# Rope columns by halves in DRAM, the swap on VectorE out of PSUM, and whole splits of the query and rope key weights

## The chip, the cores and the metric

The kernel runs on one core of one Trainium2 chip. The metric is the device time of one execution in microseconds. Before the change it was 1918.83 us, the median of three runs (1917.03 to 1919.51).

## What is computed

A decoder trunk of two layers on 256 tokens of width 2048. Layer 0 is a causal pooling mixer with a SwiGLU feed-forward network. From its result a key/value set is made once: a compressed latent of rank 512, 16 heads of keys and values of 128 columns each, and one rotary key of 64 columns that all heads share. Layer 1 is attention on that set, with low-rank queries, and a second feed-forward network. Shift, scale and gate of each sub-layer come from products of a conditioning vector with large matrices.

Of the reference, the parts that the change touches:

```
def apply_rope(t, cos, sin):
    half = t.shape[-1] // 2
    t1, t2 = t[..., :half], t[..., half:]
    return jnp.concatenate([t1 * cos - t2 * sin, t2 * cos + t1 * sin], axis=-1)

k_rope = apply_rope(h @ w_kr, cos, sin)                  # (S, 64)
q = (cq @ w_uq).reshape(B, S, N_HEADS, 128 + 64)
q_nope = q[..., :128]
q_rope = apply_rope(q[..., 128:], cos[:, :, None, :], sin[:, :, None, :])
s = q_nope @ k_nope.T + q_rope @ k_rope.T                # by head, causal, scaled, softmax
```

## The kernel before

All weights stream once from DRAM through six buffers ("raw", 8 KB a partition), nearly always as tiles of 1 MB. To keep fp32 accuracy each weight is split in two: ScalarE copies it to an upper half in fp32r (`split`, line 374), VectorE subtracts to get the lower half (line 376), and TensorE multiplies upper by upper, upper by lower and lower by upper (`proj_unit`, line 398, and `head_T`, line 1288). The loads go out on SP's queue; a raw buffer is free for the next load when VectorE has read it.

The products with the conditioning vector run in the background, on VectorE alone: one pass over a 1 MB tile with a row sum (`Part.unit`, line 211). A counter (`tick`, line 342) decides after how many weight tiles the next pass is issued: `split` counts, and so does `project_heads`, by a call of its own (line 1355). In the attention 1.5 passes go out for each of the query groups 2 to 7. When a gate's 16 passes are done, `gate_to` adds the bias (line 300) and puts a small job on the list `pending`: a transpose on TensorE (line 292), a copy on ScalarE, a DMA issued by ScalarE and one issued by POOL. The list is worked off by `flush`, which `split` calls behind its two instructions. The query split of line 1362 does not call `split`, and so does not flush.

The rope key is made at the end of `then_attention`, in a stretch whose order on TensorE, ScalarE and VectorE is written out by hand (lines 1199 to 1227). `w_kr` is loaded in rows of 64 columns (line 1176). ScalarE copies it twice, side by side, into `wkr_h` (line 1201), four subtractions make `wkr_l` (line 1217), and the matmuls of line 1208 leave the 64 rows of the rope key twice in PSUM. Then `rope_start` follows. The tables `cos_t` and `sin_t` have a row for each partition; the sign of the sine lies in a column of constants (line 81).

`rope_start` (line 840) takes the 128 x 256 product out of PSUM with ScalarE: one copy as it is (line 843) and four copies of 32 partitions each with the halves swapped (line 845). `rope_end` (line 848) multiplies the swapped one by the sine (line 849) and the other by the cosine (line 850) and adds them (line 852). For the rope key the sum goes to `krT` in two pieces of 64 partitions, one for each head of a pair, with zeros around them.

The attention works in 8 groups of two heads. `project_heads(g)` (line 1342) loads the group's columns of `w_uq`, 512 x 384 (line 1354), splits the 128 rope columns and then the 256 others, each with one ScalarE and one VectorE instruction (lines 1362 and 1363), makes the rope product with 12 matmuls (lines 1368 to 1370), calls `rope_start`, and makes the two heads' queries with 24 matmuls (line 1288). Its `finish` calls `rope_end`. In the loop at line 1448 a group runs through `probabilities` (scores on TensorE, lines 1383 to 1386; scale and mask, line 1390 on VectorE and 1388 on ScalarE; maximum, line 1393; exponentials on ScalarE, lines 1396 and 1397; reciprocal on VectorE, line 1399; the scaling by it on ScalarE, line 1400, and on VectorE, line 1401). Meanwhile the probabilities of the group before are transposed on TensorE (line 1407), copied out (line 1409) and multiplied with the values (lines 1414 and 1415), with `project_heads(g + 2)` between the two. The order of the instructions on each engine is here not written out: a scheduler puts them in order when the program is built, by their place in the program, by raised priorities (`tc.high_priority`) and by its own estimate of when each can start. On the chip each queue then keeps that order.

Of the kernel before, what the change touches and what calls it, by code (L numbers as in the profile page):

```python
# [9 lines left out]
F32 = mybir.dt.float32  # L10
# [7 lines left out]
P = 128  # L18
T = 256
# [54 lines left out]
def shape_constants():  # L74
# [6 lines left out]
    con[:, C_SIGN] = np.where(q % ROPE < HALF, -1.0, 1.0)  # L81
# [12 lines left out]
def tile_trunk(ctx: ExitStack, tc: tile.TileContext, a: dict, out: bass.AP):  # L94
# [712 lines left out]

    cos_t = const.tile([P, T], F32, name="cos_t")
# [31 lines left out]
    def rope_start(bank):  # L840

        t_ = t2k([P, 2, T])
        act.activation(t_[:, 0, :], bank, AF.Copy)
        for r in range(0, P, HALF):
            act.activation(t_[r:r + HALF, 1, :], bank[r ^ HALF:(r ^ HALF) + HALF], AF.Copy)
        return t_

    def rope_end(t_, dsts):
        dve.tensor_tensor(out=t_[:, 1, :], in0=t_[:, 1, :], in1=sin_t, op=ALU.mult)
        dve.tensor_tensor(out=t_[:, 0, :], in0=t_[:, 0, :], in1=cos_t, op=ALU.mult)  # L850
# [271 lines left out]
    def then_attention(old, banks, piece):  # L1122
# [49 lines left out]
        for j in range(2, ND):  # L1172
            w_ = w_load_of(dkv(j))
            if j == 2:
                wkr = raw_t([P, KD, ROPE])
                sync.dma_start(wkr, a["w_kr"].rearrange("(k p) n -> p k n", p=P))
# [22 lines left out]
        wkr_h, wkr_l = hl_t([P, KD, 2, ROPE]), hl_t([P, KD, 2, ROPE])  # L1199
        for i in range(2):  # L1200
            act.activation(wkr_h[:, :, i, :], wkr, AF.Copy)
# [3 lines left out]
        def key_part(n):  # L1205
            w_, i = sums[n]
            for k in range(KD):
                pe.matmul(krb[:, :T], lhsT=w_[:, k].rearrange("p i n -> p (i n)"), rhs=hkv[k // KL][:, i, k % KL, :],
# [6 lines left out]
        for ks in (slice(0, KD // 2), slice(KD // 2, KD)):  # L1215
            for i in range(2):
                dve.tensor_tensor(out=wkr_l[:, ks, i, :], in0=wkr[:, ks], in1=wkr_h[:, ks, i, :].bitcast(F32),
                                  op=ALU.subtract)
# [97 lines left out]
    rope_end(kr_t, [(slice(0, ROPE), krT[0:ROPE, 0, :]), (slice(ROPE, P), krT[ROPE:P, 1, :])])  # L1316
# [20 lines left out]
    w_uq = a["w_uq"][0]  # L1337
# [4 lines left out]
    def project_heads(g):  # L1342
        o = Heads()
        n = HG * T
        if g % 2 == 0:
# [8 lines left out]
        sync.dma_start(rq, w_uq[:, g * HG * QH:(g + 1) * HG * QH].rearrange("(k p) n -> p k n", p=P))  # L1354
        tick()
        q_h, q_l = ([t_[:, :KL * HG * NOPE].rearrange("p (k h n) -> p k h n", k=KL, h=HG),
                     t_[:, KL * HG * NOPE:].rearrange("p (k h n) -> p k h n", k=KL, h=HG)]
                    for t_ in (hl_t([P, KL * HG * QH]), hl_t([P, KL * HG * QH])))
        src = rq.rearrange("p k (h n) -> p k h n", h=HG)
# [218 lines left out]
```

## Time and profile before

| | |
|---|---|
| median of three runs | 1918.83 us (1917.03 to 1919.51) |
| the profiled execution: its time | 1918.19 us |
| its span, first to last instruction | 1916.4 us |
| mean granted TensorE clock | 0.987 |
| TensorE busy | 1862.8 us, 97% |
| VectorE busy | 1402.7 us, 73% |
| ScalarE busy | 850.2 us, 44% |

The profile is of one execution. Busy is the time in which an engine has an instruction of its own at work; PE is TensorE, PEld its weight loads, DVE VectorE, ACT ScalarE, SP the engine whose queue issues the loads. L1407 is line 1407 of the kernel. A row of the timeline begins with its start and its length in us; a wait stands behind it in brackets, with what ended it. Names such as `ps<-act,hl` are the tiles written and read. [...]

### The profile page before, as it was taken

What the parts mean: (1) busy time and instruction counts of PE and PEld (TensorE: products, weight loads), DVE (VectorE), ACT (ScalarE), POOL (GpSimd) and SP (SyncE); (2) the same over time, 40 slices, a digit from 0 to 9 for tenths busy, and PEclk for the clock granted to TensorE, in tenths of its full rate; (3) what the DMA queues carried; (4) which work ended last, traced back from release to release, by engine and by line L of the source; (5) the groups of instructions that cost most, each with busy time, mean ns of one, the idle gap of its engine ahead of it and who ended that gap; (6) DMA issues with size and microseconds to landing.
All of it is one profiled execution on the core that took longest, in us unless ns stands there. A gap on an engine that the chain in (4) does not pass through costs nothing.

```text
span 1916.4 us, 21930 instructions
## 1 busy us (share of the span) xinstructions
PE 1862.8 (97%) x8813; PEld 1507.8 (79%) x8813; DVE 1402.7 (73%) x1391; ACT 850.2 (44%) x958; POOL 26.9 (1%) x32
## 2 busy tenths in 40 slices
PE   7689999999999999999999999999999999999998
PEld 3255888888888888887889888888888888888887
DVE  2148799999788777799899966889785556645556
ACT  3125643444433334244678745634444433343343
POOL 0000000000000000002100000000000000000000
PEclk9789999999999999999999999999999999999999
DMA  9999998879998888897597775988776666665651
GB/s 399 398 418 417 368 364 333 319 299 361 357 344 332 327 330 326 332 373 274 212 371 291 293 278 194 397 318 335 260 284 240 241 240 239 249 222 205 220 198 44
DMA packets 86647, 574.98 MB, mean 300 GB/s; under 512 B 10977, under 2 KB 15505, under 8 KB 18321
## 3 DMA queue, kind: packets, MB, share of 16 engines
q1 hardware_dynamic: 86018, 570.42, 77.8%
q0 software_dynamic: 432, 3.15, 0.4%
q8 instruction: 69, 1.13, 0.2%
q14 instruction: 32, 0.26, 0.0%
q10 hardware_dynamic: 96, 0.02, 0.0%
HBM read 567.24 MB, written 6.32 MB: 299 GB/s over the span
## 4 chain that ended last, share of the span: by engine, by line
PE 69%; issue 22%; DMA 3%; DVE 3%; ACT 1%; SPq 0%; POOL 0%; POOLq 0%; DVEq 0%; ACTq 0%
PE ps L398 58%; DMA raw<-in_mod_w_dram 3%; PE ps L256 2%; PE ps L973 2%; PE ps L407 2%; PE ps L1288 2%; DVE raw L211 1%; PE ps L729 1%; PE ps L1197 1%; PE ps L540 0%; DMA raw<-in_mod_block_dram 0%; PE ps L196 0%; PE ps L948 0%; PE ps L770 0%; DVE hl L376 0%
## 5 line engine op out<-in xcount | busy, mean ns | idle before, releaser
L398 PE MATMUL ps<-hl,act 128*128 128x512 f32 x6744 | 1539.5, 390 | 1.9 <-DVE hl L376 1.0
L398 PEld LDWEIGHTS ps<-hl,act 128*128 128x128 f32 x6744 | 1263.0, 188 | 264.7 <-DVE hl L376 1.8
L376 DVE TENSOR_TENSOR hl<-raw,hl 128x2048 fp32r<-128x2048 f32 x289 | 661.1, 2289 | 253.2 <-ACT hl L374 252.5
L374 ACT ACTIVATE hl<-raw 128x2048 fp32r<-128x2048 f32 x289 | 553.1, 1918 | 647.8 <-PE ps L398 572.1
L211 DVE SCALAR_TENSOR_TENSOR raw<-raw,s_row 128x2048 f32<-128x2048 f32 x168 | 383.2, 2284 | 3.6 <-DMA raw<-in_mod_wt_dram 3.6
L256 PE MATMUL ps<-raw,s_strip 128*32 128x512 f32 x392 | 65.2, 760 | 34.6 <-DMA raw<-in_mod_w_dram 33.5
L698 DVE TENSOR_TENSOR act<-ps,act 128x512 f32<-128x512 f32 x96 | 64.5, 685 | 17.5 <-PE ps L398 17.5
L256 PEld LDWEIGHTS ps<-raw,s_strip 128*32 128x32 f32 x392 | 9.5, 121 | 70.0 <-DMA raw<-in_mod_w_dram 46.3
L784 DVE TENSOR_TENSOR x<-ps,x 128x512 f32<-128x512 f32 x32 | 22.1, 690 | 38.8 <-PE ps L398 38.8
L1288 PE MATMUL ps<-act,hl 128*128 128x256 f32 x384 | 49.6, 287 | 0.0
L1288 PEld LDWEIGHTS ps<-act,hl 128*128 128x128 f32 x384 | 48.3, 195 | 0.7 <-DVE act L1253 0.2
L407 PE MATMUL ps<-hl,act 128*128 128x512 f32 x192 | 47.0, 400 | 1.2 <-DVE act L503 1.2
L732 ACT ACTIVATE act<-ps 128x512 fp32r<-128x512 f32 x44 | 23.6, 594 | 50.0 <-PE ps L729 37.6
L407 PEld LDWEIGHTS ps<-hl,act 128*128 128x128 f32 x192 | 35.2, 188 | 10.7 <-ACT act L490 2.3
L263 DVE COPY t2k<-ps 128x256 f32<-128x256 f32 x4 | 1.7, 425 | 52.9 <-ACT t2k L262 52.9
L427 ACT ACTIVATE junk<-x 128x512 bf16<-128x512 f32 x23 | 14.5, 629 | 53.2 <-DVE x L612 37.6
L802 DVE TENSOR_TENSOR t2k<-ps,t2k 128x512 f32<-128x512 f32 x24 | 16.5, 689 | 28.5 <-PE ps L398 28.5
L798 ACT ACTIVATE t2k<-ps 128x512 f32<-128x512 f32 x24 | 14.2, 590 | 47.9 <-PE ps L398 47.9
L973 PEld LDWEIGHTS ps<-act,act 128*128 128x128 f32 x128 | 24.7, 200 | 11.6 <-issue 8.4
L696 ACT ACTIVATE act<-ps 128x512 f32<-128x512 f32 x32 | 19.1, 597 | 29.0 <-PE ps L398 28.8
L973 PE MATMUL ps<-act,act 128*128 128x256 f32 x128 | 31.9, 402 | 0.0
L733 DVE TENSOR_TENSOR act<-ps,act 128x512 fp32r<-128x512 f32 x44 | 28.1, 683 | 0.9 <-ACT act L732 0.9
(222 smaller groups left out, 911.6 us busy)
## 6 DMA issues: line engine op xcount, KB each, us to landing
raw<-in_mod_wt_dram SPq DMA_DIRECT2D x136, 1024.0 KB, 5.8
raw<-in_ffn_gate_dram SPq DMA_DIRECT2D x88, 1024.0 KB, 5.8
raw<-in_ffn_up_dram SPq DMA_DIRECT2D x88, 1024.0 KB, 5.1
raw<-in_ffn_down_dram SPq DMA_DIRECT2D x88, 1024.0 KB, 5.2
raw<-in_mod_w_dram SPq DMA_DIRECT2D x48, 1024.0 KB, 12.1
raw<-in_kv_mod_wt_dram SPq DMA_DIRECT2D x32, 1024.0 KB, 7.1
raw<-in_w_o_dram SPq DMA_DIRECT2D x16, 1024.0 KB, 6.1
raw<-in_mod_block_dram SPq DMA_DIRECT2D x8, 1024.0 KB, 12.5
```

Of the source, the lines that this page charges most:

```text
L211: dve.scalar_tensor_tensor(out=r, in0=r, scalar=1.0, in1=s_row, op0=ALU.mult, op1=ALU.mult, accum_out=self.sums[:, self.n:self.n + 1])
L256: pe.matmul(self.bank[m * STRIP:(m + 1) * STRIP, :], lhsT=weights(k), rhs=r[:, k, i, :], start=first, stop=last)
L374: hi_ins = act.activation(hi, r, AF.Copy)
L376: lo_ins = dve.tensor_tensor(out=lo, in0=r, in1=hi.bitcast(F32), op=ALU.subtract)
L398: pe.matmul(banks[tok], lhsT=t_[:, i, k, tok * P:(tok + 1) * P], rhs=w[:, k, :], start=first and n < len(part), stop=last and n >= len(ord ...
L407: pe.matmul(bank, lhsT=t_[:, i, k, tok * P:(tok + 1) * P], rhs=w[:, k, :], start=first and n == 0, stop=last and n == len(order) - 1)
L698: dve.tensor_tensor(out=part, in0=banks[tok], in1=part, op=ALU.add)
L732: act.activation(m[:, 0, :, ts_], v, AF.Copy)
L733: dve.tensor_tensor(out=m[:, 1, :, ts_], in0=v, in1=m[:, 0, :, ts_].bitcast(F32), op=ALU.subtract)
L784: dve.tensor_tensor(out=x[:, tok, js], in0=banks[tok], in1=x[:, tok, js], op=ALU.add)
L973: pe.matmul(mixed[g][:, n % 2, :], lhsT=wp[g][:, k, ns], rhs=pool_all[g // 2][:, g % 2, k, :], start=k == 0, stop=k == KL - 1)
L1288: pe.matmul(pt[:, h, :], lhsT=w(h0 + h, k), rhs=t_[:, i, k, :], start=n == 0, stop=n == 3 * KL - 1)
```

## The change

Five things change together.

- **Layout in DRAM.** `w_uq` is laid out by groups of two heads, each group with one contiguous run for a partition. Inside a group the 128 rope columns come first, ordered by halves: the first 32 of head 0, the first 32 of head 1, then the second 32 of head 0 and of head 1. `w_kr` has each half twice, 128 columns in all, and one contiguous run for a partition; it is twice as large as before.
- **Rope.** With this order the swap of halves is a swap of partitions 0 to 63 with 64 to 127. `rope_start` is now on VectorE: two products of 64 partitions with the sine, straight from PSUM, each written to the other half of the partitions, and one product of all partitions with the cosine. `rope_end` keeps the addition alone. The sign of the sine moves to the row that is read.
- **The rope key's addition** is in four pieces of 32 partitions.
- **The rope key's weights** are copied to the upper half by one ScalarE instruction and subtracted by two VectorE instructions.
- **The query weights** go through `split`: one ScalarE and one VectorE instruction of 128 x 1536, the count by `tick` and the `flush` behind them.

```diff
-    con[:, C_SIGN] = np.where(q % ROPE < HALF, -1.0, 1.0)
+    con[:, C_SIGN] = np.where(q < ROPE, 1.0, -1.0)
...
     def rope_start(bank):
         t_ = t2k([P, 2, T])
-        act.activation(t_[:, 0, :], bank, AF.Copy)
-        for r in range(0, P, HALF):
-            act.activation(t_[r:r + HALF, 1, :], bank[r ^ HALF:(r ^ HALF) + HALF], AF.Copy)
+        for r in range(0, P, ROPE):
+            other = slice(r ^ ROPE, (r ^ ROPE) + ROPE)
+            dve.tensor_tensor(out=t_[r:r + ROPE, 1, :], in0=bank[other], in1=sin_t[other], op=ALU.mult)
+        dve.tensor_tensor(out=t_[:, 0, :], in0=bank, in1=cos_t, op=ALU.mult)
         return t_

     def rope_end(t_, dsts):
-        dve.tensor_tensor(out=t_[:, 1, :], in0=t_[:, 1, :], in1=sin_t, op=ALU.mult)
-        dve.tensor_tensor(out=t_[:, 0, :], in0=t_[:, 0, :], in1=cos_t, op=ALU.mult)
         for rows, dst in dsts:
             dve.tensor_tensor(out=dst, in0=t_[rows, 0, :], in1=t_[rows, 1, :], op=ALU.add)
...
-                wkr = raw_t([P, KD, ROPE])
-                sync.dma_start(wkr, a["w_kr"].rearrange("(k p) n -> p k n", p=P))
+                wkr = raw_t([P, KD, P])
+                sync.dma_start(wkr.rearrange("p k n -> p (k n)"), a["w_kr"])
...
-        wkr_h, wkr_l = hl_t([P, KD, 2, ROPE]), hl_t([P, KD, 2, ROPE])
-        for i in range(2):
-            act.activation(wkr_h[:, :, i, :], wkr, AF.Copy)
+        wkr_h, wkr_l = hl_t([P, KD, P]), hl_t([P, KD, P])
+        act.activation(wkr_h, wkr, AF.Copy)
...
         for ks in (slice(0, KD // 2), slice(KD // 2, KD)):
-            for i in range(2):
-                dve.tensor_tensor(out=wkr_l[:, ks, i, :], in0=wkr[:, ks], in1=wkr_h[:, ks, i, :].bitcast(F32),
-                                  op=ALU.subtract)
+            dve.tensor_tensor(out=wkr_l[:, ks], in0=wkr[:, ks], in1=wkr_h[:, ks].bitcast(F32), op=ALU.subtract)
...
-    rope_end(kr_t, [(slice(0, ROPE), krT[0:ROPE, 0, :]), (slice(ROPE, P), krT[ROPE:P, 1, :])])
+    rope_end(kr_t, [(slice(r, r + HALF), krT[r:r + HALF, r // HALF % 2, :]) for r in range(0, P, HALF)])
...
         rq = raw_t([P, KL, HG * QH])
-        sync.dma_start(rq, w_uq[:, g * HG * QH:(g + 1) * HG * QH].rearrange("(k p) n -> p k n", p=P))
-        tick()
...
-        with tc.high_priority(offset=100):
-            for i, ns in ((1, slice(NOPE, QH)), (0, slice(0, NOPE))):
-                act.activation(q_h[i], src[:, :, :, ns], AF.Copy)
-                dve.tensor_tensor(out=q_l[i], in0=src[:, :, :, ns], in1=q_h[i].bitcast(F32), op=ALU.subtract)
+        sync.dma_start(rq.rearrange("p k n -> p (k n)"), w_uq[g])
+        q_h, q_l = split(rq, [P, KL, HG * QH])
         qb = ps_t()
         for k in range(KL):
-            wh, wl = (w[1][:, k].rearrange("p h n -> p (h n)") for w in (q_h, q_l))
+            wh, wl = (w[:, k, :P] for w in (q_h, q_l))
...
         t_ = rope_start(qb[:, :T])
-        head_T(o.qT, HG, lambda h, k: q_h[0][:, k, h, :], lambda h, k: q_l[0][:, k, h, :], cqT)
+        nope = [slice(HG * ROPE + h * NOPE, HG * ROPE + (h + 1) * NOPE) for h in range(HG)]
+        head_T(o.qT, HG, lambda h, k: q_h[:, k, nope[h]], lambda h, k: q_l[:, k, nope[h]], cqT)
```

## Rows read from the trace of the kernel before

**Rows 1.** The page, part 1: busy us, share of the span, instructions.

```profile
PE 1862.8 (97%) x8813; PEld 1507.8 (79%) x8813; DVE 1402.7 (73%) x1391; ACT 850.2 (44%) x958; POOL 26.9 (1%) x32
```

**Rows 2.** Busy time by stretch: rope key to latent, attention. Columns in the first line.

```profile
core 0: us, PE busy (x) PEld busy (x) DVE busy (x) ACT busy (x) POOL busy (x), PEclk, DMA share, GB/s
926.00:1009.90 83.90, 83.86 (x503) 74.06 (x502) 76.28 (x86) 63.64 (x102) 4.13 (x4) 1.00 0.85 325
1009.90:1080.00 70.10, 67.71 (x491) 64.42 (x490) 67.41 (x146) 60.06 (x160) 0.00 (x0) 0.98 0.79 286
```

**Rows 3.** Waits of TensorE, 1003 to 1100 us: total, times, longest.

```profile
PE ps L1407 <- ACT t2k L1400: 2.2, 2, 2.0
```

**Rows 4.** Timeline, 1026 to 1031 us, VectorE and TensorE.

```profile
1027.82 2.29 DVE L211 SCALAR_TENSOR_TENSOR raw<-raw,s_row 128x2048 f32<-128x2048 f32 x1
...
1030.03 0.16 DVE L1399 RECIPROCAL sm<-sm 128x2 f32<-128x2 f32 x1
...
1030.81 0.55 PE L1407 MATMUL ps<-con,t2k 128*128 128x128 f32 x3 [1.97 <-ACT t2k L1400]
```

**Rows 5.** Busy time and granted clock behind that wait, columns as in rows 2.

```profile
1031.50:1035.50 4.00, 4.00 (x23) 4.00 (x23) 4.00 (x10) 3.31 (x12) 0.00 (x0) 0.57 0.81 305
```

**Rows 6.** Timeline, 1048 to 1051 us: the same step in a later group.

```profile
1049.14 0.40 ACT L1400 ACTIVATE t2k<-t2k,sm 128x128 f32<-128x128 f32 x1
...
1049.81 0.82 PE L1407 MATMUL ps<-con,t2k 128*128 128x128 f32 x6
```

**Rows 7.** Timeline, the load of the rope key's weights and its first reader.

```profile
890.39 0.38 SPq L1176 DMA_DIRECT2D raw<-in_w_kr_dram  x1
...
927.79 2.02 ACT L1201 ACTIVATE hl<-raw 128x1024 fp32r<-128x1024 f32 x2
```

**Rows 8.** Groups of VectorE by shape: count, busy us, mean ns, idle before.

```profile
L376 DVE TENSOR_TENSOR hl<-raw,hl 128x2048 fp32r<-128x2048 f32 x289 | 661.1, 2289 | 253.2 <-ACT hl L374 252.5
L1363 DVE TENSOR_TENSOR hl<-raw,hl 128x1024 fp32r<-128x1024 f32 x8 | 9.8, 1219 | 0.0
L668 DVE TENSOR_TENSOR x<-x,t2k 128x512 f32<-128x512 f32 x8 | 5.5, 692 | 0.3
L667 DVE TENSOR_TENSOR t2k<-ps,gate 128x512 f32<-128x512 f32 x8 | 5.5, 688 | 5.9 <-PE ps L398 3.2 <-PE ps L407 2.7
...
L1363 DVE TENSOR_TENSOR hl<-raw,hl 128x512 fp32r<-128x512 f32 x8 | 5.5, 685 | 0.0
L849 DVE TENSOR_TENSOR t2k<-t2k,sin_t 128x256 f32<-128x256 f32 x9 | 3.8, 419 | 0.6 <-ACT t2k L845 0.5
...
L852 DVE TENSOR_TENSOR krT<-t2k 64x256 f32<-64x256 f32 x2 | 0.8, 414 | 0.0
```

**Rows 9.** Timeline: lower halves on VectorE and the matmuls that read them.

```profile
940.52 4.49 DVE L376 TENSOR_TENSOR hl<-raw,hl 128x2048 fp32r<-128x2048 f32 x2
...
949.84 5.92 PE L1288 MATMUL ps<-act,hl 128*128 128x256 f32 x48
...
1051.82 1.22 DVE L1363 TENSOR_TENSOR hl<-raw,hl 128x1024 fp32r<-128x1024 f32 x1
...
1068.42 0.36 PE L1368 MATMUL ps<-act,hl 128*128 128x256 f32 x1
```

**Rows 10.** DMA issues by line: count, KB each, median us to landing.

```profile
raw<-in_w_uq_dram SPq DMA_DIRECT2D x8, 768.0 KB, 6.3
```

**Rows 11.** Groups of ScalarE by shape, columns as in rows 8.

```profile
L845 ACT ACTIVATE t2k<-ps 32x256 f32<-32x256 f32 x36 | 13.5, 375 | 0.5
...
L843 ACT ACTIVATE t2k<-ps 128x256 f32<-128x256 f32 x9 | 3.4, 375 | 3.8 <-PE ps L1370 2.1 <-ACT t2k L1409 0.9 <-PE ps L1208 0.8
```

**Rows 12.** Timeline of VectorE: two pairs of instructions, one behind the other.

```profile
968.69 0.84 DVE L852 TENSOR_TENSOR krT<-t2k 64x256 f32<-64x256 f32 x2
...
984.64 0.75 DVE L560 TENSOR_TENSOR act<-t2k,act 128x256 fp32r<-128x256 f32 x2
```

**Rows 13.** Timeline: the attention's gate is summed, and later turned.

```profile
1065.22 0.17 DVE L300 TENSOR_TENSOR cols<-sums,vcol 128x16 f32<-128x16 f32 x1
...
1082.10 0.27 PE L292 MATMUL ps<-con,cols 128*16 128x128 f32 x1
```

**Rows 14.** Waits of ScalarE, 1003 to 1100 us, columns as in rows 3.

```profile
ACT t2k L843 <- PE ps L1370: 2.1, 3, 1.2
```

More of the change, by code (lines that the diff above doesn't have):

```diff
@@ L1207, in key_part @@
             for k in range(KD):
-                pe.matmul(krb[:, :T], lhsT=w_[:, k].rearrange("p i n -> p (i n)"), rhs=hkv[k // KL][:, i, k % KL, :],
+                pe.matmul(krb[:, :T], lhsT=w_[:, k], rhs=hkv[k // KL][:, i, k % KL, :],
                           start=n + k == 0, stop=n == 2 and k == KD - 1)
@@ L1336, in tile_trunk @@
     HG = 2
-    w_uq = a["w_uq"][0]
+    w_uq = a["w_uq"]
     class Heads:
@@ L1353, in project_heads @@
         rq = raw_t([P, KL, HG * QH])
-        sync.dma_start(rq, w_uq[:, g * HG * QH:(g + 1) * HG * QH].rearrange("(k p) n -> p k n", p=P))
-        tick()
[L1356 to L1359, printed above, removed]
-        with tc.high_priority(offset=100):
-            for i, ns in ((1, slice(NOPE, QH)), (0, slice(0, NOPE))):
-                act.activation(q_h[i], src[:, :, :, ns], AF.Copy)
-                dve.tensor_tensor(out=q_l[i], in0=src[:, :, :, ns], in1=q_h[i].bitcast(F32), op=ALU.subtract)
+        sync.dma_start(rq.rearrange("p k n -> p (k n)"), w_uq[g])
+        q_h, q_l = split(rq, [P, KL, HG * QH])
         qb = ps_t()
         for k in range(KL):
-            wh, wl = (w[1][:, k].rearrange("p h n -> p (h n)") for w in (q_h, q_l))
+            wh, wl = (w[:, k, :P] for w in (q_h, q_l))
             pe.matmul(qb[:, :T], lhsT=wl, rhs=cqT[:, 0, k, :], start=k == 0, stop=False)
@@ L1544, in columns @@
         return np.asarray(v).reshape(-1, P).T
-    o = {n: np.asarray(i[n]) for n in ("x", "c", "positions", "mod_w", "pool_w", "w_kr", "w_uq", "final_norm")}
+    o = {n: np.asarray(i[n]) for n in ("x", "c", "positions", "mod_w", "pool_w", "final_norm")}
     o["vectors"] = np.concatenate([columns(i[n]) for n in (
@@ L1552, in laid_out @@
     o["mod_block"] = block.transpose(0, 2, 1, 3, 4).reshape(KD // 2, P, 4 * CH)
+    w = np.asarray(i["w_uq"])[0].reshape(KL, P, H // 2, 2, QH)
+    rope = w[..., NOPE:].reshape(KL, P, H // 2, 2, 2, HALF).swapaxes(3, 4).reshape(KL, P, H // 2, 2 * ROPE)
+    w = np.concatenate([rope, w[..., :NOPE].reshape(KL, P, H // 2, 2 * NOPE)], 3)
+    o["w_uq"] = w.transpose(2, 1, 0, 3).reshape(H // 2, P, -1)
+    w = np.asarray(i["w_kr"]).reshape(KD, P, 2, 1, HALF)
+    o["w_kr"] = np.concatenate([w, w], 3).reshape(KD, P, P).transpose(1, 0, 2).reshape(P, KD * P)
     for n in ("w_dkv", "w_uk", "w_uv"):
```

## The prediction

> **What bounds the kernel now.** I read the page's busy times first: TensorE has work in 97% of the span, VectorE in 73%, ScalarE in 44% [rows 1]. So a part of this change can only matter where TensorE waits, or where another engine is nearly as full. The busy times by stretch find that place [rows 2]. From the rope key to the last query latent (926 to 1009.9 us) TensorE is busy for 83.86 of 83.90 us, and nothing that feeds it is late. In the attention, from the first query matmul to the last scores (1009.9 to 1080 us), TensorE is busy for 67.71 of 70.10 us and VectorE for 67.41: two engines are full at once, and ScalarE has 10 us to spare.
>
> TensorE's waits there come to 2.2 us in two, the longest 2.0, both for the scaled probabilities of line 1400 [rows 3]. The timeline shows the long one: VectorE works in the order of its queue, a background pass of 2.29 us (line 211) stands before the reciprocal of the second head, that starts at 1030.03, ScalarE's scaling follows it, and TensorE's transposes go on at 1030.81 after 1.97 us [rows 4]. [...] Elsewhere the chain is only just in time: in a later group ScalarE's last scaling begins at 1049.14, lasts 0.40, and TensorE turns the probabilities at 1049.81, a slack of 0.27 us [rows 6].
>
> **The change part by part.** I follow the order of the program.
>
> *Rope key's weights.* Their load grows from 512 to 1,024 KB. It is issued at 890.39 us and first read at 927.79 [rows 7]; at the 325 GB/s of the stretch that follows [rows 2] half a megabyte more is 1.6 us. The loads queued behind it on SP are as early. Without that cover of 37 us, 1.6 us would show. One ScalarE copy replaces two and two subtractions replace four, with the same elements: nothing.
>
> *Rope key itself.* Its three products now stand in VectorE's written order, ahead of the two lower halves at 940.52 us; they replace two products that ran later, and at the end four additions replace two. Three products at 0.42 [rows 8] and 0.27 for starts that can't overlap (below) put 1.5 us ahead of those two subtractions. The second one ended at 945.0; TensorE takes it from 949.84 on [rows 9]. That lead of 4.8 us hides 1.5; if it were gone, 1.5 us would show. The additions feed only the attention's scores. Nothing.
>
> *Query weights' loads.* Eight loads of 768 KB with 6.3 us to landing [rows 10] keep bytes, queue and place; only the pieces grow: nothing. Without their lead, a landing that is longer or shorter by a part of 6.3 us would show.
>
> *Query weights' split.* Before, each group costs VectorE 685 + 1,219 ns, less an overlap of some 0.09 (below). One subtraction of 1,536 elements lies halfway between 1,219 (1,024) and 2,289 (2,048): 1.75 us [rows 8]. That gives back 0.07 us a group. The rope product now waits for the whole split instead of its first third, at most 1.75 - 0.69 = 1.1 us later; but the splits run ahead of TensorE: the last is over at 1053.04, and its matmuls begin at 1068.42 [rows 9].
>
> *Query rope, ScalarE.* Five copies go: 375 + 4 x 375 ns = 1.9 us a group, 15 us in all [rows 11]. ScalarE is not what is full, and waits for it in the attention are what VectorE's order leaves, so I count no gain.
>
> *Query rope, VectorE.* Before: two products and an addition. After: two half products, a whole one and the addition, so one instruction of 0.42 more, as a 128 x 256 product takes 419 ns and half the partitions take no less (the rope key's 64-partition additions take 414) [rows 8]. The source is now PSUM. The nearest rows are lines 667 and 668, the same operation and size from PSUM and from SBUF: 688 and 692 ns [rows 8]; I count no surcharge. [...]
>
> Then the starts. Two subtractions of 128 x 256, one behind the other, take 0.75 us where two of 0.42 would take 0.84, so they overlap by 0.09. The rope key's two additions, one at partition 0 and one at 64, take 0.84 for 2 x 0.414: no overlap [rows 12]. The new products change their start partition three times in a row, so up to 3 x 0.09 = 0.27 us a group. [...]
>
> Sum for a group: 0.42 + 0.27 - 0.07 = 0.62 us, and 0.35 without the held starts. Eight groups: 5.0 us, at the lowest 2.8. I take 5.0, since the pair at partitions 0 and 64 is the nearest row. The 15 us that ScalarE loses are of another engine and pay for none of it.
>
> *The gate's rows.* The split function also sends out pending work, which the old query split did not. The attention's gate is summed at 1065.22 and turned on TensorE only at 1082.10 [rows 13], with the first output weights. The last query group's split will now send it: one 0.27 us matmul, a ScalarE copy, a DMA issue on ScalarE's queue and one on POOL's, about 15 us earlier. Their lengths stay, ScalarE has the room and POOL has nothing to do there [rows 2]. Zero if TensorE meets it after the sum; if it stands in front of a late sum, TensorE waits up to the lateness of VectorE, at most the 5.0 us above. I take zero and leave the end for the range.
>
> **Sum.** VectorE's 67.41 us in the attention become 72.4, and the stretch lasts 70.10. The 2.69 us in which it idles can be filled only in part, but if they were filled altogether the stretch still grows by 2.3 us. Outside the attention nothing. The profiled execution took 1918.19 us (span 1916.4, and 1.8 around it), 0.64 below the median of 1918.83. 1918.19 + 2.3 = 1920.5 us.
>
> **The rivals.** (a) *The background slides.* The passes of line 211 have no reader in the attention. If as much as one (2.29 us) lands behind it, VectorE's extra work is absorbed and the time stays at 1918.2. For it: in the split, VectorE is 15 us ahead of TensorE [rows 9]. Against: the passes are as old in the program as the split beside them, and at 1027.82 one came ahead of urgent work.
>
> (b) *The late reciprocal goes.* With other lengths the queue is put in another order, and the pass at 1027.82 may land behind the reciprocal: the wait, its clock and the short second wait of 0.2 us [rows 3] go: 1.97 + 1.72 + 0.2 = 3.9 less, 1914.3 us. For it: one instruction decides, and ScalarE is freed. Against: VectorE is fuller, not emptier.
>
> (c) *VectorE waits for TensorE, slower.* The first product stands in VectorE's in-order queue before the query product is done. On ScalarE the copy of line 843 waited so 2.1 us in three places, the longest 1.2 [rows 14]. Queued behind the wait are now the softmax of the previous group, the next split and a pass whose buffer the SP queue needs for the next load. Once such a wait exceeds the slack of 0.27 us [rows 6], the transposes start late; with the 2.3 of the forecast it makes 2.3 + 2.1 = 4.4, and a gap as long as that at 1028.84 costs the clock again: + 1.72. That is 6.1 us, 1924.3.
>
> (d) *The held starts don't come.* If products from PSUM overlap at their changed starts, the sum is its lower end of 2.8, and the stretch grows by 67.41 + 2.8 - 70.10 = 0.1 us: 1918.3, the same outcome as (a).
>
> **How the numbers follow.** Forecast 0.36, (a) with (d) 0.20, (b) 0.17, (c) 0.27. A measurement of this kernel can tell about 0.2%, 3.8 us, from no change: under 1915.0 counts as faster, over 1922.7 as slower. Only (b) is below, only (c) above; so 0.17, 0.56, 0.27. The time is the forecast's, 1920.5. The range takes in (b)'s 1914.3 and (c)'s 1924.3 with some of the gate's end: 1914.0 to 1925.0, leaving out a second long gap.
>
> **What would show it.** Right: three products of 0.42 us per rope from PSUM with no overlap between them, one 1.75 us subtraction a group, ScalarE's busy time down by 15 us, VectorE over 71 us between the first query matmul and the last scores, and that stretch 2 to 3 us longer in waits for line 1400 or 1409. Wrong: the stretch shorter with granted clock 1.00 throughout (b); VectorE idle on TensorE's query matmuls (c); products of clearly more than 0.45 us; or any change of TensorE's waits before 1009 or after 1100 us.

## The result, and the profile after

The changed kernel takes 1920.78 us (median of 22 runs, 1919.25 to 1923.18) against 1918.51 for the kernel before beside it (22 runs, 1914.82 to 1920.38). The ratio is 1.0014, interval 1.0008 to 1.0021: 1.5 to 4.0 us slower, and the ratio is within the 0.2% that was called no change. The forecast of 1920.5 is met. Its working isn't, as the rows show.

The profiled execution took 1919.77 us, span 1918.0. The page's part 1 answers to [rows 1]:

```profile
PE 1860.4 (97%) x8813; PEld 1508.1 (79%) x8813; DVE 1407.3 (73%) x1392; ACT 833.7 (43%) x904; POOL 28.7 (1%) x32
```

ScalarE lost 16.5 us and VectorE gained 4.6. The groups by shape, of VectorE and then ScalarE, answer to [rows 8, 11]:

```profile
L376 DVE TENSOR_TENSOR hl<-raw,hl 128x1536 fp32r<-128x1536 f32 x8 | 14.0, 1753 | 1.5 <-ACT hl L374 1.5
L846 DVE TENSOR_TENSOR t2k<-ps,sin_t 64x256 f32<-64x256 f32 x18 | 7.6, 422 | 0.4
L847 DVE TENSOR_TENSOR t2k<-ps,cos_t 128x256 f32<-128x256 f32 x9 | 3.8, 421 | 0.1
...
L374 ACT ACTIVATE hl<-raw 128x1536 fp32r<-128x1536 f32 x8 | 11.8, 1478 | 3.1 <-PE ps L1285 2.8 <-PE ps L398 0.3
```

The products from PSUM take 421 and 422 ns; those from SBUF took 419 [rows 8]. Two half products, one behind the other, take 0.86 us (timeline of VectorE), about twice the 422 ns of one: no overlap.

```profile
1059.27 0.86 DVE L846 TENSOR_TENSOR t2k<-ps,sin_t 64x256 f32<-64x256 f32 x2
```

The waits of TensorE from 926 to 1100 us answer to [rows 3]. Before there was one of 2.0 us; now there are three:

```profile
PE ps L292 <- DVE cols L300: 2.4, 1, 2.4
PE ps L1396 <- ACT t2k L1389: 1.6, 1, 1.6
PE ps L540 <- ACT t2k L530: 0.9, 1, 0.9
```

The first is the gate's transpose. The timeline has VectorE's last addition for the gate's column at 1068.35 (1065.22 before, [rows 13]), a pass of 2.29 us shortly ahead of it, and TensorE standing there:

```profile
1065.21 2.29 DVE L211 SCALAR_TENSOR_TENSOR raw<-raw,s_row 128x2048 f32<-128x2048 f32 x1
...
1068.35 0.17 DVE L300 TENSOR_TENSOR cols<-sums,vcol 128x16 f32<-128x16 f32 x1
...
1068.57 0.28 PE L292 MATMUL ps<-con,cols 128*16 128x128 f32 x1 [2.41 <-DVE cols L300]
```

The granted clock, a share of TensorE's full clock, falls to 0.57 behind that wait; behind the one of 1.65 us, at 1030, it stays at 1.00 (columns as in [rows 2]):

```profile
1030.00:1034.00 4.00, 3.97 (x33) 3.97 (x34) 3.97 (x11) 2.42 (x9) 0.00 (x0) 1.00 0.85 282
...
1068.60:1072.60 4.00, 4.00 (x22) 4.00 (x23) 3.94 (x8) 3.66 (x9) 0.00 (x0) 0.57 0.81 291
```

By the granted clock the last row loses 0.43 x 4 = 1.7 us, an estimate. The matmuls show 1.5: the 36 query matmuls from line 1356 on, up to the first of line 1403, take 5.87 us there (1068.61 to 1074.48, timeline of TensorE), and 4.40 behind the wait at 1030 (1030.33 to 1034.73). The stall that began at 1028.84 before [rows 4, 5] is still there, 1.65 us in place of 1.97, and without its low clock.

The third wait, 0.94 us at 973.88, lies where I expected no change. VectorE makes a scale column by two dependent instructions, lines 277 and 278. Before, one rope product stood between them; now it is a subtraction of 2.29 us. The kernel before, then after, VectorE:

```profile
965.65 0.17 DVE L277 SCALAR_TENSOR_TENSOR cols<-sums,vcol 128x16 f32<-128x16 f32 x1
965.74 0.42 DVE L849 TENSOR_TENSOR t2k<-t2k,sin_t 128x256 f32<-128x256 f32 x1
966.07 0.17 DVE L278 TENSOR_TENSOR cols<-cols,vcol 128x16 f32<-128x16 f32 x1
```

```profile
964.73 0.17 DVE L277 SCALAR_TENSOR_TENSOR cols<-sums,vcol 128x16 f32<-128x16 f32 x1
964.82 2.29 DVE L376 TENSOR_TENSOR hl<-raw,hl 128x2048 fp32r<-128x2048 f32 x1
967.02 0.17 DVE L278 TENSOR_TENSOR cols<-cols,vcol 128x16 f32<-128x16 f32 x1
```

ScalarE reads that column, and has no gap from there until it scales the piece that TensorE waits for (line 530). Before, then after, ScalarE:

```profile
967.51 1.02 ACT L558 ACTIVATE t2k<-ps,cols 128x256 f32<-128x256 f32 x2
```

```profile
967.29 1.02 ACT L558 ACTIVATE t2k<-ps,cols 128x256 f32<-128x256 f32 x2 [0.96 <-DVE cols L278]
```

Counted from the first rope-key matmul, the first of the two instructions starts 0.35 us later than before (34.71 against 34.36) and the second ends 2.22 us later. So 1.87 us of the lateness lies between the two, and without it ScalarE would not have waited.

**How the runs are compared.** Each kernel's times scatter over some 4 us (the kernel before from 1914.7 to 1920.4), and in the traces the time to the first projection matmul alone (line 398) lies between 168.1 and 171.8 us. So beside the medians I use three stretches of each trace, cut where TensorE starts the same matmul: the first rope-key matmul to the first query matmul (K), from there to the last weighted matmul (Q), and on to the next matmul of line 407 in the kernel before, behind the output projection (W). The other stretches agree within about 1 us. W tells when work has only crossed the border. In us, with "gap" TensorE's unbusy time in Q and "DVE W" VectorE's busy time in W:

| kernel | median | K | Q | gap | W | DVE W |
|---|---|---|---|---|---|---|
| before | 1918.51 | 78.87 | 87.57 | 2.41 | 65.19 | 43.1 |
| after | 1920.78 | 79.68 | 89.56 | 4.47 | 65.20 | 43.9 |
| after, gate's rows not sent | 1918.73 | 79.65 | 86.67 | 3.36 | 65.21 | 45.3 |
| ... and columns urgent | 1919.19 | 79.65 | 86.69 | 3.33 | 65.22 | 45.4 |
| before, gate's rows sent | 1918.94 | 78.88 | 87.72 | 2.44 | 65.21 | 43.3 |
| VectorE's rope alone | 1915.75 | 79.66 | 83.56 | 0.20 | 65.22 | 47.7 |
| ... rows sent | 1921.66 | 79.67 | 89.65 | 5.26 | 65.22 | 41.7 |
| ... rope key as before | 1915.81 | 78.83 | 84.11 | 0.40 | 65.19 | 47.7 |
| ... subtraction whole | 1918.49 | 79.64 | 86.98 | 3.63 | 65.22 | 45.3 |
| ... half products twice | 1926.06 | 81.13 | 91.49 | 6.15 | 64.29 | 48.4 |
| whole split alone | 1916.67 | 78.78 | 87.06 | 1.40 | 63.62 | 43.1 |
| after, rows one group later | 1918.42 | 79.64 | 86.66 | 3.34 | 65.22 | 45.3 |
| passes behind reciprocals | 1918.85 | 79.65 | 86.24 | 1.83 | 64.97 | 49.4 |
| ... rope key as before | 1918.79 | 78.81 | 86.53 | 2.10 | 64.99 | 49.4 |

The kernel before had medians of 1917.63, 1917.74 and 1918.32 beside the three sets of experiments (27 to 33 runs each); each ratio below is to the one beside it.

### The profile page after: what moved, and what is told of

Read it like the earlier page. It is cut to its first block, busy times and chain, and to the rows that moved or that the text cites. A ratio compares the mean times of both kernels' runs of the same rounds, so it can differ in the third digit from the quotient of the medians.

```text
span 1918.0 us, 21870 instructions
## 1 busy us (share of the span) xinstructions
PE 1860.4 (97%) x8813; PEld 1508.1 (79%) x8813; DVE 1407.3 (73%) x1392; ACT 833.7 (43%) x904; POOL 28.7 (1%) x32
## 4 chain that ended last, share of the span: by engine, by line
PE 67%; issue 22%; DVE 4%; DMA 4%; ACT 1%; POOL 0%; SPq 0%; POOLq 0%; DVEq 0%; ACTq 0%
PE ps L398 58%; DMA raw<-in_mod_w_dram 3%; PE ps L256 2%; PE ps L973 2%; PE ps L407 2%; DVE raw L211 1%; DVE hl L376 1%; PE ps L729 1%; PE ps L1197 1%; PE ps L1285 0%; DMA raw<-in_mod_block_dram 0%; PE ps L540 0%; PE ps L948 0%; PE ps L770 0%; DVE t2k L846 0%
## 5 line engine op out<-in xcount | busy, mean ns | idle before, releaser
L376 DVE TENSOR_TENSOR hl<-raw,hl 128x2048 fp32r<-128x2048 f32 (+1 forms) x297 | 675.1, 2275 | 251.7 <-ACT hl L374 251.1
L374 ACT ACTIVATE hl<-raw 128x2048 fp32r<-128x2048 f32 (+1 forms) x297 | 564.8, 1906 | 652.7 <-PE ps L398 570.5
L802 DVE TENSOR_TENSOR t2k<-ps,t2k 128x512 f32<-128x512 f32 x24 | 16.5, 689 | 28.5 <-PE ps L398 28.5
```

The lines of the kernel that those rows point to most:

```text
L374: hi_ins = act.activation(hi, r, AF.Copy)
L376: lo_ins = dve.tensor_tensor(out=lo, in0=r, in1=hi.bitcast(F32), op=ALU.subtract)
```

## The experiments

### One part undone or done at a time

**The gate's rows not sent.** In the changed kernel, the query split doesn't flush:

```
+        if send:
             flush(hi_ins, lo_ins)
-        q_h, q_l = split(rq, [P, KL, HG * QH])
+        q_h, q_l = split(rq, [P, KL, HG * QH], False)
```

> The changed kernel, with one thing undone: the query weights' split no longer works off the list of pending jobs, so the gate is again turned with the first output weights. Theory G (the gate's transpose, moved ahead of a late sum, is what costs): the wait of 2.41 us for line 300 and the low clock behind it go, some 4 us less than the changed kernel's 1920.8, that is 1916.7, with VectorE's busy time unchanged near 1407. Rival V (VectorE is too full with the rope products): the time stays at 1920.8, and waits of 2 to 4 us appear elsewhere in the attention, for line 1389 or 1398.

Ratio 1.0005, 0.9996 to 1.0013. Q falls by 2.9 us to 86.67; the wait for the gate's column and its low clock are gone (1.00 from 1065.8 to 1075.8 us), as theory G says, but the time is 2 us above G's 1916.7. Two waits are left in Q; the second was there, the first is new:

```profile
PE ps L1404 <- ACT t2k L1399: 1.7, 1, 1.7
PE ps L1397 <- ACT t2k L1390: 1.6, 1, 1.6
```

**The gate's rows sent, and nothing else.** In the kernel before, `flush(hi_ins, lo_ins)` stands behind the second part of the query split.

> The kernel before, with one thing added: after the two-part split of a query group the pending jobs are worked off. Nothing of the rope or the layout is changed. Theory G: TensorE waits for the gate's sum ahead of the last query group, 1 to 2.5 us, and up to 1.7 for the clock: 1919.5 to 1922.5 against 1918.5. Rival V: no change, 1918.5, since VectorE has no more to do than before.

Ratio 1.0003, 0.9994 to 1.0012; Q + 0.15. Theory G's wait of 1 to 2.5 us didn't come. The transpose moved from 1082 to 1069.15, and nobody waits, since the column was made at 1065.86 (timelines of VectorE and TensorE):

```profile
1065.86 0.16 DVE L300 TENSOR_TENSOR cols<-sums,vcol 128x16 f32<-128x16 f32 x1
```

```profile
1069.15 0.27 PE L292 MATMUL ps<-con,cols 128*16 128x128 f32 x1
```

So sending costs next to nothing by itself. In the changed kernel it meets a late column: up to that column, at 58.64 us after the first query matmul, VectorE does the same work in the same order with the rows sent and not sent, and TensorE is at the transpose at 56.5.

**VectorE's rope alone.** The changed kernel with the query split in two parts again, and no flush (called the rope alone below; the rope key's whole split is in it):

```
-        q_h, q_l = split(rq, [P, KL, HG * QH])
+        tick()
+        q_h, q_l = hl_t([P, KL, HG * QH]), hl_t([P, KL, HG * QH])
+        with tc.high_priority(offset=100):
+            for ns in (slice(0, P), slice(P, HG * QH)):
+                act.activation(q_h[:, :, ns], rq[:, :, ns], AF.Copy)
+                dve.tensor_tensor(out=q_l[:, :, ns], in0=rq[:, :, ns], in1=q_h[:, :, ns].bitcast(F32), op=ALU.subtract)
```

> The changed layout, the rope on VectorE and the rope key's weights split whole, but the query weights split in two parts as before (rope columns first), with no working off of pending jobs. VectorE does all the added rope work and does not get back the shorter split. Theory G: no wait for line 300, 1916.5 to 1918.5. Rival V: VectorE has the full 5.5 us more in the attention, 1921 or more.

Ratio 0.9989, 0.998 to 0.9998: some 2 us faster than the kernel before, under both theories' ranges. Q is 4.0 us shorter than before, with 0.20 us of gaps. VectorE by itself shows why. Three passes start in Q ahead of the first reciprocal, as before; the fourth, that stood ahead of the second reciprocal at 1030.03 [rows 4], starts only at 1038.38, and both reciprocals are in time.

```profile
1025.08 2.28 DVE L211 SCALAR_TENSOR_TENSOR raw<-raw,s_row 128x2048 f32<-128x2048 f32 x1
...
1027.29 0.16 DVE L1393 RECIPROCAL sm<-sm 128x2 f32<-128x2 f32 x1
...
1029.15 0.17 DVE L1393 RECIPROCAL sm<-sm 128x2 f32<-128x2 f32 x1
...
1038.38 2.28 DVE L211 SCALAR_TENSOR_TENSOR raw<-raw,s_row 128x2048 f32<-128x2048 f32 x1
```

And VectorE isn't fuller in Q, though the rope is there. These are Q and W of this kernel, by windows:

```profile
1012.25:1095.80 83.55, 83.35 (x578) 77.27 (x577) 82.66 (x176) 56.74 (x145) 0.61 (x1) 1.00 0.74 266
1095.80:1161.00 65.20, 65.20 (x290) 54.00 (x289) 47.68 (x40) 27.41 (x25) 0.00 (x0) 1.00 0.79 300
```

Over both it is busy for 130.34 us against 127.45 before: 2.9 more. But W took 4.5 more of it (43.15 before), so Q holds 1.6 less. The background slid: 11 passes start in Q and 6 in W, where it was 13 and 4.

**The column's two instructions urgent.** No sending, and `scaled_sums` at raised priority (`with urgent():`).

> The first experiment's kernel, and the two short instructions that make a scale's columns get a raised priority, so that no subtraction of 2.29 us stands between them. Theory O (the wait of 0.94 us at line 540 near 974 us in the changed kernel comes from that order, as the rope key's products no longer stand there): this wait goes, and the time is 0.8 to 1.0 us below the first experiment's. Rival: the wait comes from ScalarE's work as such; it stays, and the two kernels take the same time.

Ratio 1.0008, 0.9999 to 1.0017. The wait of 0.94 us stays, and so does its supposed cause: a subtraction of 2.28 us (967.73) still stands between the two (967.65, 969.93). This run couldn't tell; one below tells more.

**The whole split alone.** No sending, and the rope on ScalarE by the new layout: one copy of 128 partitions and four of 32, the two products in `rope_end`.

> The new layout and the whole split of the query weights, its part not sending the gate's rows, but the rope on ScalarE as before (one copy of 128 partitions, four of 32, both products on VectorE from SBUF). Run with VectorE's rope and no sending, the stretch from the first query matmul to the last weighted matmul took 86.67 us; with VectorE's rope and the split in two parts 83.56; before it took 87.57. Theory 'order': the whole split costs nothing by its length; it shifts the order in which VectorE's programme has the gate's passes and the reciprocals, and here a pass stands ahead of the first head's reciprocal, as it did with 83.56, and none between the second head's maximum and its reciprocal. Then no wait of TensorE of 1.5 us or more with a reciprocal behind a pass, the stretch 83.5 to 85.0, the time 1915.5 to 1917.5. Theory 'length': a copy of 1.47 us and a subtraction of 1.75 us in one piece hold up what stands behind them, 3.1 us in the stretch; then 87.57 + 3.1 = 90.7 and a time of 1921 to 1922. The stretch ahead of it, from the first rope-key matmul to the first query matmul: 78.9, as before, since the rope key's rope is on ScalarE again (theory 'columns', below); 79.7 if the whole split of the rope key's weights or the four additions are what cost there.

Ratio 0.9995, 0.9986 to 1.0004. Q is 87.06, far from the 90.7 of 'length', and 1.6 us of it is seven matmuls of the first output product that crossed the border: Q and W together are 2.1 us shorter than before. TensorE waits for the scaled probabilities 1.3 us in three, the longest 0.8; the low clock is gone (1.00 from 1009 to 1101 us). With ScalarE's rope the whole split costs nothing. K is 78.78, with four additions and the rope key's whole split in it, as 'columns' asked. 'Order' asked for 83.5 to 85.0 and is half a microsecond off with the border counted in.

**The rope key as before.** The rope alone, but the rope key's by ScalarE's five copies, the products ahead of the additions (subtractions, for the sign).

> The kernel with VectorE's rope and the query split in two parts (1915.75 us), but the rope key's rope on ScalarE as before; its four additions of 32 partitions become subtractions, for the table's sign. Theory 'columns': the 0.94 us wait ahead of the first piece's transposes comes because VectorE's two instructions that make a scale column have a subtraction of 2.29 us between them, where before a rope product of 0.42 stood. With the rope key's products back there it goes: the stretch from the first rope-key matmul to the first query matmul 78.9 instead of 79.66, and no wait over 0.2 us in it. Rival: the four additions or the products' own time (1.3 us more on VectorE) make it; then 79.6 and the wait stay. The attention's stretch: 83.5 to 84.5, its rope and split are unchanged. Time 1914.5 to 1915.8.

Ratio 0.9989, 0.998 to 0.9998. K is 78.83 and the wait is gone, with a rope product again between the two instructions, and all four additions still there:

```profile
966.27 0.17 DVE L277 SCALAR_TENSOR_TENSOR cols<-sums,vcol 128x16 f32<-128x16 f32 x1
966.35 0.42 DVE L1317 TENSOR_TENSOR t2k<-t2k,sin_t 128x256 f32<-128x256 f32 x1
966.69 0.17 DVE L278 TENSOR_TENSOR cols<-cols,vcol 128x16 f32<-128x16 f32 x1
```

So neither the four additions nor the whole split of the rope key's weights cost K its 0.8. The run doesn't separate the place between the two instructions from the products' own time, since the first of the two also comes 1.3 us earlier than with the rope alone; the 0.35 and 1.87 us read from the traces above do. K and Q lose 3.5 us against before; against the rope alone K gains 0.8, Q loses 0.55, and the median shows neither.

**The rope alone, and sent.** `flush` behind the second part of the split.

> The kernel with VectorE's rope and the query split in two parts (1915.75 us), with the gate's rows sent after the split, as the change does. Sending early cost the kernel before 0.15 us in the attention's stretch, and 2.9 us where the whole split stood beside it. Theory 'late column': sending early moves the gate's transpose into an earlier place of TensorE's order, and it costs only as much as VectorE's addition that makes the gate's column ends after TensorE gets there; in this kernel VectorE is 0 to 4 us ahead of where it is with the whole split, so that the transpose waits 0 to 1 us and the stretch is 83.6 to 84.6, the time 1915.6 to 1916.8. Rival 'sending': it costs about 2.4 us plus 0.5 of low clock with VectorE's rope, whatever the split; then the stretch is 86 to 86.5 and the time 1918.3 to 1918.8.

Ratio 1.0026, 1.0017 to 1.0035. Both sizes are missed: the wait is 4.99 us, and Q 89.65. VectorE's column comes 59.5 us after the first query matmul (1070.77 - 1011.24), 0.7 us later than in the changed kernel, where I had it 0 to 4 us earlier; and TensorE, with no stall ahead, is there at 54.6, 1.9 us earlier.

```profile
1070.60 0.17 DVE L300 TENSOR_TENSOR cols<-sums,vcol 128x16 f32<-128x16 f32 x1
```

```profile
1070.82 0.38 PE L292 MATMUL ps<-con,cols 128*16 128x128 f32 x1 [4.99 <-DVE cols L300]
```

The price of sending is the distance between the column and TensorE, and I had sized it by the wrong kernel: what made Q short (no stall) brings TensorE there early, and the column no earlier.

**Only the subtraction whole.** The rope alone, with ScalarE's copy in two parts and VectorE's subtraction in one.

> The kernel with VectorE's rope, no sending, ScalarE's copy in two parts, VectorE's subtraction in one. In two parts both: 83.56 us from the first query matmul to the last weighted matmul; in one both: 86.67. Theory 'order': in this programme a pass of the gate stands between the second head's maximum and its reciprocal, as with 86.67 and before; so the wait of 1.6 to 2.0 us for that reciprocal is back and the stretch takes 85.5 to 87, the time 1917.6 to 1919. Rival 'copy': it is ScalarE's copy in one piece that makes the 3.1 us (the second 1.69 us wait stood behind ScalarE's work); then the stretch is 83.6 to 84.2 and the time 1915.7 to 1916.3.

Ratio 1.0006, 0.9997 to 1.0015. Q is 86.98, all of the 3.1 us and more: it is the subtraction, not the copy. A pass is back between the two reciprocals:

```profile
1027.64 0.16 DVE L1393 RECIPROCAL sm<-sm 128x2 f32<-128x2 f32 x1
...
1028.83 2.28 DVE L211 SCALAR_TENSOR_TENSOR raw<-raw,s_row 128x2048 f32<-128x2048 f32 x1
...
1031.05 0.16 DVE L1393 RECIPROCAL sm<-sm 128x2 f32<-128x2 f32 x1
```

The two waits are 1.8 us each. The other one stands behind ScalarE: a split of an output weight (1.91 us from 1076.16) lies ahead of the copy of the transposed probabilities at 1078.12.

### The causes by themselves

**The gate's rows one group later.** The changed kernel whole, one number changed:

```
-            pending.append((0, spread))
+            pending.append((1 if name == "mla" else 0, spread))
```

> The changed kernel whole, but the rows of this one gate are sent one query group later. Sent after the split (1920.78 us), TensorE reached the gate's transpose 2.41 us before VectorE's addition that makes the gate's column had ended, and 1.8 us of low clock stood behind; in the kernel with VectorE's rope and the split in two parts TensorE waited 4.99 us there. Theory 'late column': VectorE's column ends 58.8 to 59.6 us after the first query matmul with the rope on VectorE, 55 before, and the transposes of the early sending are reached at 54.6 to 56.5; one group later they are reached some 8 us later, and nobody waits. Then the stretch from the first query matmul to the last weighted matmul falls from 89.56 to what it is without sending, 86.7 (its other two waits, 1.65 and 1.69, stay), and the time is 1918.3 to 1919.3. Rival: sending costs by itself, by what it adds to the queues; then a wait of 2 us or more stays at the transpose or at a transfer and the stretch is 88.5 or more, 1920.5 or more.

Ratio 1.0002, 0.9993 to 1.0011. Q is 86.66, 2.9 us less, and the median 2.4 less than the changed kernel's. The column (1072.07) is as late as ever; TensorE is not there before 1084.48. 'Late column' foresaw this, but the run is not a second proof of it: behind the last query group the next place to send is the first output weights, and all four engines run the same instructions in the same order as with the rows not sent. It repeats that run. What carries 'late column' is the column's place, the same whether the rows are sent or not (58.6 us here, and 59.3 with the rope alone), and waits as long as TensorE is early: 2.41 and 4.99 us, and none in the kernel before, where the column comes at 55.1 us and TensorE at 58.4.

**The half products twice.** The rope alone, with `for _ in range(2):` around each half product.

> The kernel with VectorE's rope and the query split in two parts (83.56 us from the first query matmul to the last weighted matmul; 1915.75 us), with the two half products of the rope done twice: 0.86 us more on VectorE in each of eight query groups and once for the rope key, 6.9 us in the attention, more than the 5.0 that the change put on it. The stretch from the last weighted matmul to the handover has 17.5 us of VectorE to spare. Theory 'full' (the forecast's): VectorE bounds the attention, and the stretch grows by 5 to 7 us, the time 1920.5 to 1922.5. Theory 'order': the gate's passes go later into that room, and only where a pass or a product comes ahead of what TensorE waits for does it cost; here no pass stands between a second head's maximum and its reciprocal in the first pairs, so the stretch is 83.5 to 85.5, the time 1915.7 to 1917.7.

Ratio 1.0041, 1.0028 to 1.0053. The median is of 5 runs. 'Order' was wrong; 'full' was right in kind and too low: Q grows by 7.9 us for 6.9 us of work, K by 1.5, and the time is 3.6 us above its range. The windows of Q and W:

```profile
1013.56:1105.05 91.49, 85.34 (x582) 78.29 (x581) 89.66 (x190) 57.14 (x145) 0.61 (x1) 1.00 0.64 231
1105.05:1169.30 64.25, 64.25 (x286) 53.23 (x285) 48.38 (x41) 27.06 (x25) 0.00 (x0) 1.00 0.81 316
```

W takes only 0.7 us more than with the rope alone, and 11 passes start in Q again, though W has 15.9 us of VectorE left. Nothing more slid, and the next microsecond on VectorE was paid in full. In K the wait of 0.94 us is now 2.41, although only an addition of 0.40 us stands between lines 277 and 278: here line 277 itself starts 3.4 us later. So what counts is when the second instruction ends, and what falls between the two is one way to make it late.

**The passes behind the reciprocals.** No sending, whole split; in the attention each pass is put behind the latest group's second reciprocal when the program is ordered:

```
+            with tc.issue_after(divided[-1]) if divided else nullcontext():
                 dve.scalar_tensor_tensor(out=r, in0=r, scalar=1.0, in1=s_row, op0=ALU.mult, op1=ALU.mult,
...
+            divided.append(heads[g].divided)
```

> VectorE's rope, the whole split, no sending (86.67 us from the first query matmul to the last weighted matmul, 1918.73 us), and in the attention each of the gate's passes is put in the programme behind the second reciprocal of the heads before it. Nothing is added or taken away. Theory 'order': both waits, 1.65 us for the second head's reciprocal and 1.69 us ahead of the weighted matmuls, come from what stands ahead on VectorE, and the 1.65 with its low clock goes; the stretch 83.4 to 84.6, the time 1915.5 to 1916.8. Theory 'length': it is the whole split's copy or subtraction that stands in the way; then the stretch stays at 86 to 87 and the time at 1918.2 to 1919.2. The first wait of 0.94 us ahead of the pieces' transposes stays, the stretch ahead 79.65.

Ratio 0.9997, 0.9988 to 1.0006. The late reciprocal is cured (1028.84, with the pass at 1028.92 behind it), and so is the wait of 1.7 us. Yet Q loses only 0.4:

```profile
PE ps L1407 <- ACT t2k L1402: 0.7, 2, 0.4
PE ps L295 <- DVE cols L303: 0.6, 1, 0.6
PE ps L1400 <- ACT t2k L1393: 0.3, 1, 0.3
```

These make 1.6 of the 2.7 us by which Q is longer than with the rope alone; the rest is spread in starts of matmuls that come later by less than such a row shows. A forced order takes away the two waits and brings many small ones. So a pass ahead of a reciprocal does stall TensorE. Whether the rest of the price is the whole subtraction's or the forced order's, this run can't tell: VectorE idles for 4.7 us of Q, against 1.2 with the whole split unforced and 0.9 with the rope alone, and no run has the forced order with the split in two parts.

**The same, with the rope key as before.**

> The kernel with the gate's passes behind the reciprocals (VectorE's rope for the queries, whole split, no sending), and the rope key's rope on ScalarE as before. Theory 'order' and theory 'columns' together: no wait of TensorE over 0.5 us from the first rope-key matmul to the last weighted matmul, the two stretches 78.8 and 83.4 to 84.4, 3.3 us or more under the kernel before in their sum (166.44), the time 1914.8 to 1916.0. If one of the two is wrong, its wait is back, 0.94 in the first stretch or 1.6 with its clock in the second, and the time 1916 to 1919.

Ratio 1.0, 0.9991 to 1.0009. K is 78.81, so the wait in K goes a second time; Q is 86.53, and 'order' misses again, by 2 us.

## Why the number was right and the working wrong

In the traces K and Q grow by 0.8 + 2.0 = 2.8 us; the medians differ by 2.3, the forecast said 2.3. But the parts are four, and the one that I predicted isn't among them:

| step | Q, us | forecast |
|---|---|---|
| VectorE's rope (before to rope alone) | -4.0 | +2.3, with the split |
| whole split (to rows not sent) | +3.1 | in the sum, -0.07 a group |
| sending (to after) | +2.9 | zero, end 5.0 |
| the rope key, in K | +0.8 | nothing |

The steps are taken in this order, and their prices depend on it: sending costs 0.15 us in the kernel before and 6.1 beside the rope alone.

**The step that failed** is "VectorE's 67.41 us in the attention become 72.4, and the stretch lasts 70.10": I let VectorE's sum set the length of the stretch. With the same work on VectorE and only the gate's rows not sent, Q is 0.9 us shorter than before, and with the rope alone 4.0. What TensorE lacks in the changed kernel stands in two waits (2.41 and 1.65 us) and one low clock (0.57 over 4 us), not in VectorE's sum.

The sum was mis-sized too. The 5.0 us are 3.4 in the traces (127.45 us in Q and W before, 130.85 after), nearer to the lower end of 2.8; and the last scores end at 1082.26, not at 1080. From the first query matmul to their end, before and then after:

```profile
1010.16:1082.26 72.10, 69.71 (x503) 66.19 (x502) 69.41 (x151) 60.82 (x161) 0.00 (x0) 0.98 0.76 278
```

```profile
1009.70:1083.68 73.98, 69.67 (x503) 66.37 (x502) 71.60 (x147) 46.73 (x116) 0.61 (x1) 0.98 0.76 272
```

By my rule 69.41 + 3.4 against 72.10 would have made 0.7 us. The 1.9 us that came, with VectorE over 71, are close to the sign that I gave for being right. But the wait for line 1400 (1389 now) got shorter, what is new in Q is the wait for the gate's column, and the wait at 973.88 is among the signs of being wrong. That the number was met is luck: a bound that did not hold, sized too high, stood in for a gain and three prices that were not in the sum.

Rival (a) did not come in the changed kernel. As many passes start in Q and in W as before (a pass is two instructions, Q in the first row and W in the second; before, then after):

```profile
1010.16:1097.72 87.56, 29.80 (x26) 0.98 0.77 285
1097.72:1162.92 65.20, 9.19 (x8) 1.00 0.72 271
```

```profile
1009.70:1099.27 89.57, 29.77 (x26) 0.98 0.75 271
1099.27:1164.46 65.19, 9.19 (x8) 1.00 0.76 268
```

It came with the rope alone, where two passes slid and not one, and (b) beside it: the pass left its place ahead of the second reciprocal, and (b)'s 1.97 + 1.72 + 0.2 = 3.9 is near the 4.0 measured. I gave these two 0.20 and 0.17 as alternatives; both came true for the rope, and the rest of the change took them back. A bound by VectorE there is: with 6.9 us more on it beyond the rope alone, Q paid 7.9. I placed it some microseconds too early.

No run shows the 1.72 us of clock in (b) and (c): it is 0.43 of the 4 us of [rows 5], an estimate. In its place the traces show 1.47: the 39 matmuls from the end of the wait of 1.97 us take 6.17 us (1030.81 to 1036.98), and 4.70 (1030.03 to 1034.73) behind the 1.65 us of the changed kernel, where the clock is 1.00. Nor does a gap as long always bring the low clock, as (c) took it (last section).

**The gate's rows** at zero were mis-sized: 2.41 us and 1.5 of clock by the matmuls (1.7 by the granted clock), 2.9 net of the wait of 1.7 us that stands in Q when they aren't sent. The condition stood in the text ("if it stands in front of a late sum"), and the lateness too ("at most the 5.0 us"). I took zero because the sum came 17 us ahead of the transpose; but the transpose would move and the sum as well. Sent with the first output weights, the price is gone.

**The rope key** at "nothing": its own chain was hidden, as written. The cost came mainly through what it left: without its product, the place between two dependent instructions went to a subtraction of 2.29 us. I priced the instructions moved, not the place that they vacate.

**The query split**: 1,753 ns for the 1.75 forecast, and TensorE's first use wasn't late. The size was right; that one piece in place of two moves what stands around it was not in the sum. It costs 3.1 us with VectorE's rope and nothing with ScalarE's. VectorE of the changed kernel with the rows not sent shows one part: the whole subtraction stands ahead of the first reciprocal, where the rope alone has its third pass, and the pass comes ahead of the second.

```profile
1026.33 1.75 DVE L376 TENSOR_TENSOR hl<-raw,hl 128x1536 fp32r<-128x1536 f32 x1
1027.99 0.16 DVE L1389 RECIPROCAL sm<-sm 128x2 f32<-128x2 f32 x1
...
1029.18 2.29 DVE L211 SCALAR_TENSOR_TENSOR raw<-raw,s_row 128x2048 f32<-128x2048 f32 x1
...
1031.39 0.16 DVE L1389 RECIPROCAL sm<-sm 128x2 f32<-128x2 f32 x1
```

**What was right**: three products of 0.42 us with no surcharge for PSUM (421 and 422 ns against the 419 from SBUF [rows 8]), no overlap at changed starts (0.86 us for two half products), ScalarE 16.5 us less for 15 and no gain from it by itself. Rival (c) didn't come: none of VectorE's waits from 1003 to 1100 us is for a query matmul.

**Left open**: why the scheduler's order comes out so with the whole subtraction, and whether it can be cured. In the traces its two waits are the price: TensorE's gaps in Q are 3.36 us with it and 0.20 without, and TensorE's busy time is the same. A pass ahead of the second reciprocal makes one; the other stands behind ScalarE's split, and is argued from the order there. With both taken away by a forced order most of the time stays, in other places. The best of the kernels is the rope alone, with the rope key on either engine: 1915.75 and 1915.81 us, a ratio of 0.9989 to the kernel before.

## What to carry to other kernels

Where a scheduler orders the queues, a change's price is not its instructions' lengths: look for what can fall into each place that it opens (between two dependent instructions, ahead of a reciprocal), and do the parts one by one, since here a gain of 4.0 us and losses of 3.1 and 2.9 added up to a small number. Before an engine that is 96% busy is called the bound, ask how much of its work has no reader in the stretch and a stretch behind it with room; once no more of it slides, each microsecond counts in full, even with room left behind (here 7.9 us for 6.9, with 15.9 left in W). Work that is sent earlier must be measured against the engine that feeds it, at its place after the change.

## What was not expected of the hardware

Gaps of nearly the same length, and of the same, left TensorE's clock in different states. Behind 1.82 us (the subtraction whole) the granted clock stayed at 1.00; behind the 1.97 before it was 0.57 over 4 us [rows 5], and 0.50 in each microsecond from 1032 to 1035. The first, by windows:

```profile
1031.80:1035.80 4.00, 3.96 (x33) 3.96 (x34) 3.96 (x12) 2.51 (x9) 0.00 (x0) 1.00 0.94 277
```

And 2.41 us came out both ways: 0.57 behind the gate's transpose of the changed kernel, 1.00 behind the wait in K of the half products done twice, at 977.75:

```profile
PE ps L540 <- ACT t2k L530: 2.4, 1, 2.4
```

```profile
977.80:981.80 4.00, 4.00 (x22) 3.38 (x23) 4.00 (x8) 4.00 (x10) 0.00 (x0) 1.00 1.02 395
```

So the length of a gap alone did not decide. No run here shows what did.

Where the clock fell, the price did not grow with the gap. By the granted clock it is an estimated 1.7 us behind 1.97 and behind 2.41, and behind 4.99 (the rope alone, sent) 0.38 x 4 = 1.5. TensorE's busy time in Q (Q less gap) is longer by 1.80 us before than with the rope alone, by 1.78 after than with the rows not sent, and by 1.03 with the rope alone sent than not sent. Behind the 4.99, by windows:

```profile
1070.80:1074.80 4.00, 3.98 (x23) 3.98 (x24) 4.00 (x3) 2.88 (x7) 0.00 (x0) 0.62 0.94 293
```
